# A two-layer hybrid decoder: part of the opening's modulation moved from VectorE to column tiles of TensorE

## The chip, the core and the metric

The kernel runs on one core of a Trainium2 chip. The core has five engines with a queue of instructions each: TensorE (PE, matmuls and, as PEld, their weight loads), VectorE (DVE), ScalarE (ACT), GpSimd (POOL) and SyncE (SP), which here mostly starts DMA transfers. The metric is device time in microseconds (us); lower is better.

## The reference

One sequence of 256 tokens with 2048 features goes through two layers. Each layer has six modulation vectors from a condition `c`, then a mixer (sliding-window attention beside an RWKV-7 recurrence) and a feed-forward part, each followed by a layer norm. Cut to what the change touches:

```python
cond = silu(c)                                                  # (1, 2048)
for l in range(2):
    mod = (cond @ w_ada[l] + b_ada[l]).reshape(1, 6, 1, 2048)   # 2048 x 12288 weights
    sh_m, sc_m, gt_m, sh_f, sc_f, gt_f = [mod[:, i] for i in range(6)]
    u = x * (1 + sc_m) + sh_m
    proj = u @ w_in[l]                                          # attention and RWKV columns
    ...
    mix = concat(y_attn, y_rwkv) @ w_out[l]
    x = layer_norm(alpha * x + gt_m * mix)
    u = x * (1 + sc_f) + sh_f
    ...                                                         # SwiGLU
    x = layer_norm(alpha * x + gt_f * ffn)
```

A modulation is thus a product of one row (2048 values of `cond`) with a matrix: 16 row steps of 128 rows each, all in f32.

## The kernel before, in words

**Weight products.** TensorE works on f32r pairs: `steps` (L414) loads a tile of weights as `raw`, splits it into `hi` (ACT, L430) and `lo` (DVE, L431), and `stream` (L452 to L455) or `tstream` (L464 to L466) issues three matmuls for each block. There are four `raw` tiles.

**The opening.** Nothing can be projected before the first two modulations, shift and scale of layer 0's mixer. `parts` (L1352) cuts the 2048 columns into five parts of 512, 512, 512, 256 and 256. For each, `ada_first` (L340) loads 16 row steps of both modulations at once (512 KB a step in the wide parts, 256 KB in the narrow ones, eight `ast` tiles in rotation) and adds them up on DVE: L351 for the first, L353 for the others (`acc = ast * cond + acc`, with a value of `cond` for each partition). `acc` then holds 128 partial sums for every column. `ada_sums` (L311) adds up the partitions: blocks of 128 columns are transposed on PE (L322), ACT sums each row of the result (L326, with the sum as a second output), and DVE adds the bias (L329). In the opening the transposes of both modulations take the same PSUM bank in turn, because `front` (L513) holds the other. `make_u` (L396) then transposes x (L404) and makes `u`, and `front` multiplies that part's columns with the weights of three groups of columns (`rk`, `lb` and eight blocks in `acc`).

**Later modulations.** `ada_steps` (L251) makes the other 20 units of 1024 columns, a few row steps at a time among the weight streams (L263 and L265 on DVE, then `ada_sums`). The two units of layer 0's mixer gate instead go through `ada_direct` (L276) while attention runs: each row step is a product on PE with `cond`'s 128 values broadcast to 32 columns, in four column tiles of 32, so that one bank collects four quarters of the row (L285, `gv`); ACT copies it (L299), two transposes bring it back to columns (L303), DVE adds the bias (L306).

**The mixer's order** is written out by hand in `ORDER`, one string for each layer: D, R, A, I, C, E are the steps of RWKV head group 0 to 3 (E ends with the group's two tiles of y), Q the attention projections, X opens the attention, a, b, c its three steps for each group of heads, w and z the output projection of attention and RWKV tiles. As long as `left` isn't empty, a finished y is written to DRAM (`keep_y`, L602); `have_y` (L612) brings it back through one tile `ysc`/`yf` (L616) and splits it (L509 on ACT, L510 on DVE). In layer 0 that holds for the tiles 8 to 11 (groups 0 and 1), fetched in z0 and z1.

Within these orders a planner, which simulates the engines, places the instructions of each queue. The constants' loads, the zero fills of `tinv` (L1379), the first `w2a2` (L644, L645) and the first rows of `ada_steps` (L261) have free tiles from the start and no order against the opening's rows.

Of the kernel before, what the change touches and what calls it, by code (L numbers as in the profile page):

```python
# [10 lines left out]
F32 = mybir.dt.float32  # L11
# [8 lines left out]
P = 128  # L20
# [21 lines left out]
    "D0 R0 A0 D1 I0 R1 C0 E0 Q1 A1 I1 D2 R2 A2 Q0 D3 C1 R3 E1 I2 A3 X Q2 a0 a1 b0 C2 a2 b1 c0 E2 a3 c1 I3 b2 b3 c2 c3 w0 C3 w1 w2 E3 z0 z1 z2 z3 w3",  # L42
    "D0 R0 A0 D1 R1 I0 C0 Q2 E0 A1 I1 D2 R2 A2 D3 Q1 C1 R3 E1 A3 I2 Q0 X a0 a1 b0 b1 c0 C2 I3 a2 b2 E2 a3 c1 b3 c2 c3 w0 C3 z0 w1 w2 E3 z1 z2 z3 w3",
)
PARTS = (4, 4, 4, 2, 2)
LAG = 2
WB = (4, 3, 2)
RED = 1
# [17 lines left out]
IDLE = {"ada": 0, "first": 0, "dec": (0, 0), "ffn": (11, 6), "mix": 8}  # L66
# [3 lines left out]
def hybrid_trunk_kernel(  # L70
# [92 lines left out]
    def prm(l, nm, i, n=1):  # L163
        o = PC[nm] + i
        return par[l][:, o // P, o % P:o % P + n]
# [5 lines left out]

    def setup(sp, l, half, behind=None):
# [78 lines left out]
    def ada_steps(l, mod, c0):  # L251

        src = w_ada[l].rearrange("(j p) n -> p j n", p=P)
        n0 = mod * D + c0
        if direct[0]:
            yield from ada_direct(l, mod, c0, src[:, :, n0:n0 + 1024])
            return
        acc = adap.tile([P, 1024], F32, tag="aacc", name="aacc")
        for j in range(KT):
            t = adap.tile([P, 1024], F32, tag="ast", name="ast", bufs=2)  # L260
            dma(t, src[:, j, n0:n0 + 1024])  # L261
# [12 lines left out]
        yield  # L274

    def ada_direct(l, mod, c0, src):  # L276
# [24 lines left out]
        b = bank()  # L301
        for i in range(2):
            PE.transpose(b[:, i * P:(i + 1) * P], row[:, i * P:(i + 1) * P], ident)  # L303
        col = mod * KT + c0 // P
        bv = b[:, 0:T].rearrange("p (i q r) -> p q i r", q=4, r=32)
        V.scalar_tensor_tensor(mods[l][:, col:col + 8].rearrange("p (q i) -> p q i", q=4), bv[:, :, :, 0], 1.0 if mod in (1, 4) else 0.0,  # L306
                               prm(l, "b_ada", col, 8).rearrange("p (q i) -> p q i", q=4), ALU.add, ALU.add)
# [3 lines left out]
    def ada_sums(l, mod, c0, blocks, idle=0):  # L311

        col = mod * KT + c0 // P
        n = len(blocks)
        sm = adap.tile([P, 8], F32, tag="asum", name="asum", bufs=2)
        for q in range(0, n, 4):
            b = bank()
            if q == 0:
                warm(b, idle)
            m = min(4, n - q)  # L320
            for i in range(m):
                PE.transpose(b[:, i * P:(i + 1) * P], blocks[q + i], ident)  # L322
            for i in range(m):
                bi = b[:, i * P:(i + 1) * P]
                if RED:
                    S.activation(bi, bi, AF.Copy, accum_out=sm[:, q + i:q + i + 1])  # L326
            if not RED:
                V.reduce_sum(sm[:, q:q + m], b[:, 0:m * P].rearrange("p (i k) -> p i k", k=P), axis=AX.X)
        V.scalar_tensor_tensor(mods[l][:, col:col + n], sm[:, 0:n], 1.0 if mod in (1, 4) else 0.0,  # L329
                               prm(l, "b_ada", col, n), ALU.add, ALU.add)  # L330
        if mod in (2, 5):
            row = adap.tile([8, P], F32, tag="arow", name="arow", bufs=2)[0:n]
            rb = bank()
            PE.transpose(rb[0:n, 0:P], mods[l][:, col:col + n], ident)
            S.copy(row, rb[0:n, 0:P])
            dma(gates[l, mod // 3, c0 // P:c0 // P + n], row)
# [3 lines left out]
    def ada_first(pool, c0, w):  # L340
# [3 lines left out]
        jj = 512 // w  # L344
        for j0 in range(0, KT, jj):
# [3 lines left out]
            for j in range(jj):  # L349
                if j0 + j == 0:  # L350
                    V.tensor_scalar_mul(acc, t[:, j], cond[:, 0:1])  # L351
                else:
                    V.scalar_tensor_tensor(acc, t[:, j], cond[:, j0 + j:j0 + j + 1], acc, ALU.mult, ALU.add)  # L353
            yield
        for m in range(2):
            ada_sums(0, m, c0, [acc[:, m, i * P:(i + 1) * P] for i in range(w // P)], IDLE["ada"] if m == 0 and c0 + w == D else 0)

# [182 lines left out]
    def mixer(l, us, mixp, feeds):  # L540
# [99 lines left out]
        def decays(g):  # L640
# [3 lines left out]
            dma(w2a2[0:64, :], rwkv_w2[l, :, gsl])  # L644
            dma(w2a2[64:128, :], rwkv_a2[l, :, gsl])  # L645
# [428 lines left out]
        for op in ORDER[l].split():  # L1074
# [9 lines left out]
            elif op[0] == "I":  # L1084
                invert(n, st[n], nscr[n])
            elif op[0] == "C":
# [262 lines left out]
    with tc.tile_pool(name="pro", bufs=1) as pp:  # L1349
        xv = x[0].rearrange("(t p) d -> p t d", p=P)  # L1350

        def parts():  # L1352
# [25 lines left out]
            for t in tinv:  # L1378
                dma(t.rearrange("e s t -> (e s t)").rearrange("(p n) -> p n", p=P), zt)  # L1379
# [38 lines left out]
```

## Time and profile before

| | us |
|---|---|
| median of 3 runs (2666.31 to 2670.81) | 2669.09 |
| profiled execution, its own time | 2671.02 |
| its span | 2669.0 |
| PE busy | 2518.3 |
| DVE busy | 1803.2 |
| ACT busy | 1186.1 |

The granted TensorE clock of the profiled execution was 0.974 on the mean. In a timeline's row stand the start, the duration, engine, line, operation, output and inputs, shape, the count of merged instructions and, in brackets, idle time before it with what ended it. In a row of waits: who waited for whom, the total in us, how often, and the longest. Starts are us from the span's start.

### The profile page before, as it was taken

What the parts mean: (1) busy time and instruction counts of PE and PEld (TensorE: products, weight loads), DVE (VectorE), ACT (ScalarE), POOL (GpSimd) and SP (SyncE); (2) the same over time, 40 slices, a digit from 0 to 9 for tenths busy, and PEclk for the clock granted to TensorE, in tenths of its full rate; (3) what the DMA queues carried; (4) which work ended last, traced back from release to release, by engine and by line L of the source; (5) the groups of instructions that cost most, each with busy time, mean ns of one, the idle gap of its engine ahead of it and who ended that gap; (6) DMA issues with size and microseconds to landing.
All of it is one profiled execution on the core that took longest, in us unless ns stands there. A gap on an engine that the chain in (4) does not pass through costs nothing.

```text
span 2669.0 us, 42270 instructions
## 1 busy us (share of the span) xinstructions
PE 2518.3 (94%) x15619; PEld 2090.0 (78%) x15619; DVE 1803.2 (68%) x2439; ACT 1186.1 (44%) x2023; POOL 147.2 (6%) x368
## 2 busy tenths in 40 slices
PE   3798998999999999999999999989899999999997
PEld 3797885677788888788888877867788888888887
DVE  7977766578777777676788776565855455545456
ACT  2464454335444444444444544544444443344442
POOL 1002122000000000000000023120000000000000
PEclk9899998999999999999999999989999999999999
DMA  9977668688998889888878685425655655566654
GB/s 370 361 214 250 198 186 264 204 327 294 326 337 297 302 303 314 292 301 298 300 250 304 196 274 160 121 58 185 218 188 186 194 186 194 195 191 188 192 188 147
DMA packets 336384, 637.51 MB, mean 239 GB/s; under 512 B 59510, under 2 KB 126514, under 8 KB 334642
## 3 DMA queue, kind: packets, MB, share of 16 engines
q1 hardware_dynamic: 333170, 629.05, 71.2%
q0 software_dynamic: 1280, 2.62, 0.4%
q10 hardware_dynamic: 1728, 3.15, 0.3%
q8 instruction: 122, 2.00, 0.3%
q14 instruction: 84, 0.69, 0.1%
HBM read 622.08 MB, written 12.62 MB: 238 GB/s over the span
## 4 chain that ended last, share of the span: by engine, by line
PE 76%; DMA 12%; DVE 6%; ACT 2%; issue 2%; POOL 1%; SPq 0%; DVEq 0%; ACTq 0%; POOLq 0%
PE acc L453 19%; PE acc L452 19%; PE acc L455 19%; DMA ast<-in_w_ada_dram 6%; PE acc L466 3%; PE acc L465 2%; PE acc L464 2%; DMA raw<-in_w_gate_up_dram 2%; DVE lo L431 2%; DVE aacc L265 1%; PE acc L977 1%; PE m L801 1%; PE mb L1288 1%; DMA raw<-in_w_in_dram 1%; PE aa L733 1%
## 5 line engine op out<-in xcount | busy, mean ns | idle before, releaser
L430 ACT CAST hi<-raw 128x1024 fp32r<-128x1024 f32 (+2 forms) x728 | 758.0, 1044 | 1078.8 <-PE acc L455 816.7
L431 DVE TENSOR_TENSOR lo<-raw,hi 128x1024 fp32r<-128x1024 f32 (+2 forms) x728 | 879.0, 1211 | 501.7 <-PE acc L453 342.8
L453 PE MATMUL acc<-lo,u 128*128 128x512 f32 x1568 | 514.9, 395 | 11.9 <-DVE lo L431 11.9
L455 PE MATMUL acc<-hi,u 128*128 128x512 f32 x1568 | 506.2, 391 | 0.0
L452 PE MATMUL acc<-hi,u 128*128 128x512 f32 x1568 | 459.3, 394 | 2.1 <-ACT sg L1281 1.6
L265 DVE SCALAR_TENSOR_TENSOR aacc<-ast,cond,aacc 128x1024 f32<-128x1024 f32 x270 | 345.4, 1279 | 115.7 <-DMA ast<-in_w_ada_dram 114.4
L453 PEld LDWEIGHTS acc<-lo,u 128*128 128x128 f32 x1568 | 293.1, 189 | 79.3 <-DVE lo L431 20.0
L452 PEld LDWEIGHTS acc<-hi,u 128*128 128x128 f32 x1568 | 295.2, 189 | 65.5 <-ACT sg L1281 2.5
L455 PEld LDWEIGHTS acc<-hi,u 128*128 128x128 f32 x1568 | 295.0, 188 | 61.7 <-issue 0.3
L453 PE MATMUL acc<-lo,ht 128*128 128x512 f32 (+1 forms) x720 | 243.9, 378 | 3.1 <-DVE lo L431 3.0
L455 PE MATMUL acc<-hi,ht 128*128 128x512 f32 (+1 forms) x720 | 242.2, 375 | 0.0
L452 PE MATMUL acc<-hi,ht 128*128 128x512 f32 (+1 forms) x720 | 217.0, 376 | 0.0
L464 PE MATMUL acc<-u,hi 128*128 128x256 f32 x720 | 200.9, 287 | 1.4 <-ACT hi L430 1.4
L465 PE MATMUL acc<-u,hi 128*128 128x256 f32 x720 | 201.1, 287 | 0.0
L466 PE MATMUL acc<-u,lo 128*128 128x256 f32 x720 | 188.9, 289 | 4.0 <-DVE lo L431 3.8
L453 PEld LDWEIGHTS acc<-lo,ht 128*128 128x128 f32 x720 | 134.9, 188 | 30.1 <-DVE lo L431 6.4
L455 PEld LDWEIGHTS acc<-hi,ht 128*128 128x128 f32 x720 | 135.6, 188 | 24.3
L452 PEld LDWEIGHTS acc<-hi,ht 128*128 128x128 f32 x720 | 134.7, 188 | 24.4
L464 PEld LDWEIGHTS acc<-u,hi 128*128 128x128 f32 x720 | 139.9, 194 | 4.4 <-issue 1.8
L465 PEld LDWEIGHTS acc<-u,hi 128*128 128x128 f32 x720 | 139.6, 194 | 2.8 <-issue 1.6
L466 PEld LDWEIGHTS acc<-u,lo 128*128 128x128 f32 x720 | 130.8, 193 | 8.9 <-DVE lo L431 5.7
L1128 POOL TENSOR_TENSOR brs<-brs,mhalf 128x1 f32<-128x1 f32 x8 | 7.1, 893 | 1713.1 <-DVE brs L1127 777.6
(358 smaller groups left out, 2943.6 us busy)
## 6 DMA issues: line engine op xcount, KB each, us to landing
ast<-in_w_ada_dram SPq DMA_DIRECT2D x368, 512.0 KB
raw<-in_w_gate_up_dram SPq DMA_DIRECT2D x704, 256.0 KB
raw<-in_w_down_dram SPq DMA_DIRECT2D x176, 512.0 KB
raw<-in_w_in_dram SPq DMA_DIRECT2D x82, 512.0 KB
raw<-in_w_out_dram SPq DMA_DIRECT2D x64, 512.0 KB
raw<-in_w_in_dram SPq DMA_DIRECT2D x120, 256.0 KB
ast<-in_w_ada_dram SPq DMA_DIRECT2D x32, 256.0 KB
lnw<-in_ln_w_dram SPq DMA_DIRECT2D x4, 1024.0 KB
```

The costliest lines, as they stand in the source:

```text
L265: ins = V.scalar_tensor_tensor(acc, t, cond[:, j:j + 1], acc, ALU.mult, ALU.add)
L430: S.copy(h, fl)
L431: ins = V.tensor_tensor(r, fl, h.bitcast(F32), ALU.subtract)
L452: PE.matmul(bt, lhsT=xh, rhs=hi[:, c0:c0 + w], start=st, stop=False)
L453: PE.matmul(bt, lhsT=xh, rhs=lo[:, c0:c0 + w], start=False, stop=False)
L455: PE.matmul(banks[t][q][:, 0:w], lhsT=xl, rhs=hi[:, c0:c0 + w], start=False, stop=sp_)
L464: PE.matmul(bt, lhsT=hi[:, c0:c0 + w], rhs=xh, start=st and opens, stop=False)
L465: PE.matmul(bt, lhsT=hi[:, c0:c0 + w], rhs=xl, start=False, stop=False)
L466: PE.matmul(bt, lhsT=lo[:, c0:c0 + w], rhs=xh, start=False, stop=sp_ and closes)
L733: PE.matmul(aas[h][:, cc * P:(cc + 1) * P], lhsT=bkc[hs, cc, :], rhs=ar[hs, cc, :], start=True, stop=True)
L801: PE.matmul(m1[BH[i], e * CH:(e + 1) * CH], lhsT=st[i]["am"][e // NCH][BH[i], e % NCH, 0:CH], rhs=yt[BH[i], e, :], start=True, stop=True)
L977: PE.matmul(sbs[par_][:, j * w:(j + 1) * w], lhsT=qT[hs, j, n * P:(n + 1) * P], rhs=kT[hs, 0:w], start=True, stop=True)
```

## The change

Each part of the opening adds 12 of its 16 row steps on DVE as before; the last four are products on PE in four column tiles of 32, into the bank `gv`. When both are done, `ones` products add the 128 partitions of `acc` to that bank, ACT copies the row of it, transposes bring it to columns and DVE adds the bias of both modulations. This sum by ones also takes the place of transposes and ACT sums in the 18 later units made on DVE (8 transposes and 8 ACT sums each before; 4 products, one copy and 2 transposes after). Besides:

- `fetch` puts the first `w2a2` loads, the zero fills of `tinv` and the first two row loads of `ada_steps` behind the last row load of the opening;
- layer 0's order fetches the parked y early (`y0` after E2, `y1` after I3);
- layer 1's order has C2 and I3 ahead of a2, `b1` after a2, `b2` after c1, and z0 after E3.

```diff
 ORDER = (
-    "... X Q2 a0 a1 b0 C2 a2 b1 c0 E2 a3 c1 I3 b2 b3 c2 c3 w0 C3 w1 w2 E3 z0 z1 z2 z3 w3",
-    "... X a0 a1 b0 b1 c0 C2 I3 a2 b2 E2 a3 c1 b3 c2 c3 w0 C3 z0 w1 w2 E3 z1 z2 z3 w3",
+    "... X Q2 a0 a1 b0 C2 a2 b1 c0 E2 y0 a3 c1 I3 y1 b2 b3 c2 c3 w0 C3 w1 w2 E3 z0 z1 z2 z3 w3",
+    "... X a0 a1 b0 C2 I3 a2 b1 c0 E2 a3 c1 b2 b3 c2 c3 w0 C3 w1 w2 E3 z0 z1 z2 z3 w3",
 )
+ROWS_PE = {512: 4, 256: 4}
...
+    def fetch(dst, src, later=True):
+        ins = dma(dst, src)
+        if later:
+            tc.add_manual_dep(ins.ins, lead[0], order, reason="behind the first modulation rows")
...
 (ada_steps)
-            dma(t, src[:, j, n0:n0 + 1024])
+            fetch(t, src[:, j, n0:n0 + 1024], j < 2 and not done)
...
-        ada_sums(l, mod, c0, [acc[:, i * P:(i + 1) * P] for i in range(8)])
+        ada_sums(l, c0, acc, (mod,), 8)
+        if mod in (2, 5):
+            gate_row(l, mod, c0, 8)
...
+    def row_blocks(acc, w):
+        return [acc[:, q // 2, q % 2 * w:(q % 2 + 1) * w] if len(acc.shape) == 3 else acc[:, q * w:(q + 1) * w] for q in range(4)]
+
+    def add_rows(gv, t, w, weights, first, last):
+        for q, blk in enumerate(row_blocks(t, w)):
+            PE.matmul(gv[32 * q:32 * q + 32, 0:w], lhsT=weights.to_broadcast([P, 32]), rhs=blk, start=first, stop=last)
+
+    def ada_sums(l, c0, acc, mods_, n, gv=None):
+        w = len(mods_) * n * P // 4
+        first = gv is None
+        if first:
+            gv = bank()
+        add_rows(gv, acc, w, ones, first, True)
+        row = row_blocks(acc, w)[0]
+        S.copy(row, gv[:, 0:w])
+        place(l, c0, row, mods_, w)
+
+    def place(l, c0, row, mods_, w):
+        b, m = bank(), w // P
+        for i in range(m):
+            PE.transpose(b[:, i * P:(i + 1) * P], row[:, i * P:(i + 1) * P], ident)
+        bv = b[:, 0:w].rearrange("p (i q r) -> p q i r", q=4, r=32)
+        nq = 4 // len(mods_)
+        for k, mod in enumerate(mods_):
+            col = mod * KT + c0 // P
+            V.scalar_tensor_tensor(mods[l][:, col:col + nq * m].rearrange(...), bv[:, k * nq:(k + 1) * nq, :, 0],
+                                   1.0 if mod in (1, 4) else 0.0, prm(l, "b_ada", col, nq * m).rearrange(...), ALU.add, ALU.add)
...
 (ada_first)
+        cut = KT - ROWS_PE[w]
+        gv = None
...
-                if j0 + j == 0:
+                k = j0 + j
+                if k >= cut:
+                    gv = gv or bank()
+                    add_rows(gv, t[:, j], w // 2, cond[:, k:k + 1], k == cut, False)
+                elif k == 0:
                     V.tensor_scalar_mul(acc, t[:, j], cond[:, 0:1])
...
-        for m in range(2):
-            ada_sums(0, m, c0, [acc[:, m, i * P:(i + 1) * P] for i in range(w // P)], ...)
+        ada_sums(0, c0, acc, (0, 1), w // P, gv)
...
 (decays)
-            dma(w2a2[0:64, :], rwkv_w2[l, :, gsl])
-            dma(w2a2[64:128, :], rwkv_a2[l, :, gsl])
+            fetch(w2a2[0:64, :], rwkv_w2[l, :, gsl], l + g == 0)
+            fetch(w2a2[64:128, :], rwkv_a2[l, :, gsl], l + g == 0)
...
+            elif op[0] == "y":
+                have_y([8 + 2 * n, 9 + 2 * n])
...
-                dma(t.rearrange("e s t -> (e s t)").rearrange("(p n) -> p n", p=P), zt)
+                fetch(t.rearrange("e s t -> (e s t)").rearrange("(p n) -> p n", p=P), zt)
```

`ada_direct` ends in `place` too, and `gate_row` is the end of the old `ada_sums` (one transpose, a copy and a store for the gates), moved into a function.

More of the change, by code (lines that the diff above doesn't have):

```diff
@@ L41 @@
 ORDER = (
[L42 to L43 removed]
+    "D0 R0 A0 D1 I0 R1 C0 E0 Q1 A1 I1 D2 R2 A2 Q0 D3 C1 R3 E1 I2 A3 X Q2 a0 a1 b0 C2 a2 b1 c0 E2 y0 a3 c1 I3 y1 b2 b3 c2 c3 w0 C3 w1 w2 E3 z0 z1 z2 z3 w3",
+    "D0 R0 A0 D1 R1 I0 C0 Q2 E0 A1 I1 D2 R2 A2 D3 Q1 C1 R3 E1 A3 I2 Q0 X a0 a1 b0 C2 I3 a2 b1 c0 E2 a3 c1 b2 b3 c2 c3 w0 C3 w1 w2 E3 z0 z1 z2 z3 w3",
 )
 PARTS = (4, 4, 4, 2, 2)
+ROWS_PE = {512: 4, 256: 4}
 LAG = 2
 WB = (4, 3, 2)
[L48 removed]
 AR = (3, 7)
@@ L65 @@
 TWO_PI = 2.0 * math.pi
-IDLE = {"ada": 0, "first": 0, "dec": (0, 0), "ffn": (11, 6), "mix": 8}
+IDLE = {"first": 0, "dec": (0, 0), "ffn": (11, 6), "mix": 8}
 @with_exitstack
@@ L300, in ada_direct @@
         turn[:] = 1, 1
[L301 to L307, printed above, removed]
+        place(l, c0, row, (mod,), T)
@@ L308, in ada_direct @@
         done.add((l, mod, c0 // 1024))
         yield
-    def ada_sums(l, mod, c0, blocks, idle=0):
-        col = mod * KT + c0 // P
[L314 to L336, printed above, removed]
@@ new lines, in place @@
+    def place(l, c0, row, mods_, w):
[6 more added lines that the diff above has]
+            col = mod * KT + c0 // P
+            V.scalar_tensor_tensor(mods[l][:, col:col + nq * m].rearrange("p (q i) -> p q i", q=nq), bv[:, k * nq:(k + 1) * nq, :, 0],
+                                   1.0 if mod in (1, 4) else 0.0,
+                                   prm(l, "b_ada", col, nq * m).rearrange("p (q i) -> p q i", q=nq), ALU.add, ALU.add)
@@ L338, in hybrid_trunk_kernel, with gate_row @@
+    def gate_row(l, mod, c0, n):
+        col = mod * KT + c0 // P
+        row = adap.tile([8, P], F32, tag="arow", name="arow", bufs=2)[0:n]
+        rb = bank()
+        PE.transpose(rb[0:n, 0:P], mods[l][:, col:col + n], ident)
+        S.copy(row, rb[0:n, 0:P])
+        dma(gates[l, mod // 3, c0 // P:c0 // P + n], row)
     lead = []
@@ L349, in ada_first @@
             for j in range(jj):
-                if j0 + j == 0:
+                k = j0 + j
[3 more added lines that the diff above has]
+                elif k == 0:
                     V.tensor_scalar_mul(acc, t[:, j], cond[:, 0:1])
                 else:
-                    V.scalar_tensor_tensor(acc, t[:, j], cond[:, j0 + j:j0 + j + 1], acc, ALU.mult, ALU.add)
+                    V.scalar_tensor_tensor(acc, t[:, j], cond[:, k:k + 1], acc, ALU.mult, ALU.add)
             yield
-        for m in range(2):
-            ada_sums(0, m, c0, [acc[:, m, i * P:(i + 1) * P] for i in range(w // P)], IDLE["ada"] if m == 0 and c0 + w == D else 0)
+        ada_sums(0, c0, acc, (0, 1), w // P, gv)
     done = set()
```

## The prediction

> **What bounds the kernel now.** I read the page first, then the stages, then the waits of each stage.
>
> ```profile
> span 2669.0 us, 42270 instructions
> PE 2518.3 (94%) x15619; PEld 2090.0 (78%) x15619; DVE 1803.2 (68%) x2439; ACT 1186.1 (44%) x2023; POOL 147.2 (6%) x368
> ```
>
> TensorE (PE) is busy for all but 151 us, so a change pays where it takes PE's waits away or starts PE sooner. The largest loss is the opening; its stages follow (columns: PE, weight loads, DVE, ACT, POOL busy us with counts, granted clock, DMA share, GB/s).
>
> ```profile
> 60.00:100.00 40.00, 27.63 (x206) 25.76 (x205) 37.53 (x38) 14.96 (x33) 0.00 (x0) 0.89 1.05 392
> 100.00:130.00 30.00, 27.17 (x189) 26.14 (x190) 27.74 (x45) 15.76 (x43) 0.00 (x0) 0.81 1.04 341
> 134.60:162.50 27.90, 27.85 (x227) 27.58 (x227) 15.72 (x31) 15.12 (x31) 1.03 (x4) 0.94 0.63 176
> 44.00:162.50 118.50, 98.55 (x727) 94.71 (x727) 98.26 (x132) 53.12 (x118) 1.03 (x4) 0.90 0.94 321
> ```
>
> To 130 us the DMA is full and DVE works 65.3 of 70 us; from 134.6 PE has no gap and the DMA is at 0.63. PE's front runs from 44 to 162.5 us: 727 instructions at 27.85/227 = 0.123 us need 89 us, so 29 us are lost, 20 idle and the rest to a clock of 0.90. What PE waited for there:
>
> ```profile
> PE mb L322 <- DVE aacc L353: 8.7, 2, 4.6
> PE mb L404 <- ACT mb L326: 5.2, 3, 1.7
> PE lb L464 <- ACT u L410: 2.2, 2, 1.1
> PE mb L322 <- ACT mb L326: 1.7, 1, 1.7
> ```
>
> 15.6 us of the 20 are waits on the modulation: its row sum on DVE, and the column sums on ACT.
>
> ```profile
> 128.24 6.26 DVE L353 SCALAR_TENSOR_TENSOR aacc<-ast,cond,aacc 128x512 f32<-128x512 f32 x8
> 134.65 0.41 PE L322 MATMUL mb<-ident,aacc 128*128 128x128 f32 x2 [4.12 <-DVE aacc L353]
> 144.59 0.38 PE L322 MATMUL mb<-ident,aacc 128*128 128x128 f32 x2
> ```
>
> At the end DVE is the one that lags: eight rows back to back, with PE's queue standing 4.12 us at the transposes, though the full DMA stage ended at 130. The second modulation's transposes follow only at 144.6.
>
> **The change part by part.** *Row steps to PE.* DVE's rows of the opening:
>
> ```profile
> L353 DVE SCALAR_TENSOR_TENSOR aacc<-ast,cond,aacc 128x1024 f32<-128x1024 f32 x45 | 57.7, 1282 | 7.9 <-DMA ast<-in_w_ada_dram 7.4
> ...
> L353 DVE SCALAR_TENSOR_TENSOR aacc<-ast,cond,aacc 128x512 f32<-128x512 f32 x30 | 22.5, 749 | 0.7 <-DVE mods L329 0.2
> ```
>
> DVE loses 12 x 1.28 + 8 x 0.75 = 21.4 us. PE gains 20 product rows of four column tiles. The direct unit of layer 0 issues the same form, 256 columns wide:
>
> ```profile
> 443.90 0.64 PE L285 MATMUL gv<-ast,cond 128*32 128x256 f32 x8
> 444.46 0.72 PE L977 MATMUL acc<-qT 64*128 64x128 f32 x8
> ...
> 485.65 1.50 PE L285 MATMUL gv<-ast,cond 128*32 128x256 f32 x24
> 487.08 0.71 PE L836 MATMUL mr<-bkt,ah 64*128 64x128 f32 x4
> ```
>
> One row of four tiles (eight records) holds PE 0.56 us alone and 1.43/3 = 0.48 in a run. The 12 wide rows cost 12 x 0.56 = 6.7. The 8 rows of 128 columns have no row: half to all of 0.56; nearer to half, as the work is halved, so 0.35 and 2.8. With five sums by ones (3 x 0.56 + 2 x 0.35 = 2.4) and eight row transposes (1), that is 13 us.
>
> *Sums.* Old and new forms:
>
> ```profile
> 36.29 1.12 PE L322 MATMUL mb<-ident,aacc 128*128 128x128 f32 x4 [20.86 <-DVE aacc L353]
> 41.92 1.11 PE L404 MATMUL mb<-ident,xt 128*128 128x128 f32 x4 [1.72 <-ACT mb L326]
> ```
>
> ```profile
> L299 ACT COPY grow<-gv x2: 372/372/372, 467.5 to 517.5; 128x256 f32<-128x256 f32 x2
> L303 PE MATMUL mb<-ident,grow x4: 271/272/273, 469.5 to 522.3; 128*128 128x128 f32 x4
> ```
>
> ```profile
> 734.89 1.04 PE L322 MATMUL mb<-ident,aacc 128*128 128x128 f32 x8
> 735.69 0.71 PE L453 MATMUL acc<-lo,u 128*128 128x512 f32 x2
> ```
>
> Eight transposes hold PE 0.80 us, so the opening's 32 give back 3.2: PE's work rises by 13 - 3.2 = about 10 us, from 89 to 99. From the last DVE row to the transposes of x the old sum takes 41.92 - 36.29 = 5.6 us, because both modulations go through one bank in turn; the new one is a product (0.64), a copy (0.37), two overlapping transposes (0.27 each) and two small DVE steps, with handoffs about 2.3, an estimate. That saves 3.3 us at each of five sums. The 18 later units trade 0.80 us of transposes for one sum (0.56) and two transposes (0.2): nothing on PE, -0.2 to +0.3 each, and 3 us less of ACT, which does not bound those stages. New is that the two transposes wait for an ACT copy; the L303 row, the same pair, showed no wait of PE. I take +1 for all 18 (bounds -4 to +5).
>
> *Transfers moved behind the last opening row:*
>
> ```profile
> 24.23 0.35 SPq L1379 DMA_DIRECT2D tinv<-zt  x1
> ...
> 30.02 0.81 SPq L261 DMA_DIRECT2D ast<-in_w_ada_dram  x2
> ...
> 41.62 0.34 SPq L261 DMA_DIRECT2D ast<-in_w_ada_dram  x1
> ```
>
> ```profile
> ast<-in_w_ada_dram SPq DMA_DIRECT2D x56, 512.0 KB
> ...
> tinv<-zt SPq DMA_DIRECT2D x2, 260.0 KB
> ```
>
> Three rows of the next unit (the third needs the first one's buffer), two zero fills and two small loads: 1.57 + 0.53 and some 0.1 = 2.2 MB, 5.6 us of a full DMA at 390 GB/s. They go to where the DMA is at 0.63: of 28 us some 10 are free, so I charge nothing. Without that cover they would push the last w_in tiles back by 5.6 us. On SP they were ahead of opening rows; now only w_in tiles stand behind them.
>
> *Opening, sum.* The first matmul moves from 44 to about 44 - 5.6 - 3.3 = 35. Work is 99. Of the 29 lost I expect 20: the DVE waits (8.7) mostly go, as DVE no longer lags and the products fill the gap ahead of each sum; the ACT waits shrink by half. The front would end at 35 + 99 + 20 = 154 instead of 162.5. Bounds: with all 29 still lost 163 (no gain), with the modulation's 15.6 all gone 148 (-14). I take -8. What is late next is PE itself.
>
> The Trainium skill ("TensorE: Matmul & The Clock Gate", What's actually happening) says that the array runs at half clock by default and at full clock only after about 3.4 us of activity. The rows agree in kind (0.81 and 0.89 before 130 us). By that rule products in idle gaps would also save clock, and the front would end some 5 us sooner than this sum.
>
> *The early y0 and y1 of layer 0.* Heads 0 and 1 were parked in DRAM; the kernel fetches them just as PE wants them:
>
> ```profile
> 531.11 5.32 SPq L616 DMA_DIRECT2D yf<-yd  x2
> ...
> 530.65 0.50 PE L452 MATMUL acc<-hi,yl 128*128 128x512 f32 x1 [2.31 <-ACT yl L509]
> ...
> 535.67 0.50 PE L452 MATMUL acc<-hi,yl 128*128 128x512 f32 x1 [0.42 <-ACT yl L509]
> ...
> 538.72 0.50 PE L452 MATMUL acc<-hi,yl 128*128 128x512 f32 x1
> ...
> 544.45 0.53 PE L452 MATMUL acc<-hi,yl 128*128 128x512 f32 x1 [2.72 <-ACT yl L509]
> ...
> 548.90 0.39 PE L452 MATMUL acc<-hi,yl 128*128 128x512 f32 x1
> ```
>
> Idle 2.31 + 0.42 + 2.72 = 5.4 us. The twelve matmuls after the second, short wait take 538.72 - 535.67 = 3.05 us; those after the first take 535.67 - 0.42 - 530.65 = 4.6 and those after the last 548.90 - 544.45 = 4.45, so 3 more go to the slow clock: 8.4 us in all, bounds 0 and -8.4. Hoisting puts four casts, four subtractions and four loads (each waiting for one buffer, on SP among the direct unit's row loads) into the attention, where PE waits on chains: +1. I take -7 and +1.
>
> *Order of layer 1.* I3 and C2 move ahead of a2 and b1, z0 to the end. Waits there that this could touch:
>
> ```profile
> PE m L808 <- issue: 2.1, 1, 2.1
> PE m L801 <- DVE den L1000: 1.6, 1, 1.6
> ```
>
> I take -1 of these 3.7, with +3 as the other bound: z0 no longer fills PE between C3 and w1.
>
> *Sum:* -8 - 7 + 1 + 1 - 1 = -14. The profiled execution took 2671.0 us (span 2669.0 and 2 around it), 1.9 above the median of 2669.1. 2671 - 14 = 2657, from the median 2655; I forecast **2656**. PE is the busy engine after the opening (94% of the span), so what is won there should stay.
>
> **The rivals.** *The opening gives nothing.* Products stand in PE's in-order queue until their row lands, 1.35 us apart (0.52 MB at 390 GB/s). If PE stops for the four landings of the parts 2 and 3, 8 x 1.35 = 10.8 us, what was idle is idle again. Behind them stand the w_in matmuls of the part before and the sum, for which ACT's u waits. For it: the DMA is full. Against it, the direct unit's waits for its row loads, 0.6 us at most:
>
> ```profile
> PE gv L285 <- DMA ast<-in_w_ada_dram: 1.5, 3, 0.6
> ```
>
>  Its time: 2656 + 8 = 2664.
>
> *The y waits stay*, because the planner or the single buffer leaves the loads late: 2656 + 7 = 2663.
>
> *The clock follows the work:* the front regains the 9 us of slow clock too, 2656 - 7 = 2649.
>
> *Slower: PE stands at the row copy.* In each of the 18 units the two transposes may wait for the copy (0.37) behind a cast on ACT:
>
> ```profile
> L430 ACT CAST hi<-raw 128x1024 fp32r<-128x1024 f32 (+2 forms) x728 | 758.0, 1044 | 1078.8 <-PE acc L455 816.7
> ```
>
> 18 x (0.37 + 1.04) = 25 us, 2681. It outweighs the gain from 0.8 us per unit on. Against it: the L303 pair without a wait, and the planner has weight products to put between.
>
> **How the numbers follow.** Forecast 0.55, opening nothing 0.18, y waits stay 0.08, clock 0.11, copy 0.08. The range is 2644 to 2668: the lower end is the clock rival with the upper bounds of the y and layer 1 terms, the upper end the opening rival with the +4 of later units; beyond it lies the slower rival. A difference under 0.2% (5.3 us) can't be told from none. Forecast and clock fall on faster, the two partial rivals lie at that bound, and the copy on slower: 0.77 faster, 0.15 same, 0.08 slower.
>
> **What would show it.** The last opening row on DVE before 126 us and no wait of PE on it over 2 us; the front's end near 154; no wait on yl before z0 and z1; transposes after a row copy with no idle time before them. It is wrong if PE idles ahead of gv products in the opening, if the front ends after 160, or if ACT copies head PE's waits.

## The result and the profile after

The changed kernel took **2687.5 us** (median of 7 runs, 2676.8 to 2696.5), the kernel before 2666.3 beside it (7 runs). The ratio is 1.0070 (95% interval 1.0052 to 1.0088): some 19 us **slower**, where the prediction had 2656 and a range up to 2668. Below, ratios are turned into us with 2667 us, about the kernel before in every comparison.

The page of the profiled execution after:

```profile
span 2686.0 us, 42325 instructions
...
PE 2535.2 (94%) x15831; PEld 2083.2 (78%) x15831; DVE 1782.3 (66%) x2419; ACT 1137.1 (42%) x1694; POOL 147.3 (5%) x368
```

DVE and ACT lost work as planned (21 and 49 us), PE's busy time grew by 17, and so did the span. To see where, the spans of both traces are cut into five stages: the opening up to the end of the last product on the `lb` columns; layer 0's mixer up to the first product of its feed-forward part; that part up to the first product of layer 1's front; layer 1's front and mixer; the second feed-forward part and the end.

| us | opening | mixer 0 | feed-forward 0 | mixer 1 | feed-forward 1 | span |
|---|---|---|---|---|---|---|
| before | 157.4 | 465.9 | 768.0 | 526.3 | 751.4 | 2669.0 |
| after | 151.4 | 475.1 | 780.2 | 526.1 | 753.2 | 2686.0 |
| difference | -6.0 | +9.2 | +12.2 | -0.2 | +1.8 | +17.0 |

**The opening** came out about as forecast (-6.0 for -8). Stages of after, then of before (columns as in the prediction's table of stages), cut from the first product to the last on the `lb` and `rk` columns:

```profile
38.30:151.70 113.40, 99.46 (x828) 87.98 (x828) 79.38 (x108) 41.00 (x64) 0.99 (x4) 0.94 0.96 347
```

```profile
44.00:157.70 113.70, 93.75 (x686) 90.03 (x686) 93.90 (x125) 48.76 (x110) 1.03 (x4) 0.89 0.95 330
```

The stage starts 5.7 us sooner and is as long as before: 142 more instructions on PE, but 14 us idle instead of 20 and a clock of 0.94 instead of 0.89. DVE's last rows in after stand at

```profile
114.65 4.68 DVE L375 SCALAR_TENSOR_TENSOR aacc<-ast,cond,aacc 128x512 f32<-128x512 f32 x6
```

and PE's waits between 38 and 152 us are short:

```profile
PE lb L485 <- ACT u L431: 3.7, 3, 1.5
PE acc L485 <- ACT hi L451: 2.6, 2, 1.4
PE mb L425 <- DVE mods L341: 2.4, 2, 2.0
PE mb L319 <- ACT u L431: 2.1, 1, 2.1
```

The DVE row sum, 8.7 us of waits before, is gone from the list.

**The first feed-forward stage** is where the forecast saw next to nothing and 12 us went. The stretch from 640 to 1390 us lies within it in both. After, and then before:

```profile
640.00:1390.00 750.00, 733.76 (x3383) 595.23 (x3382) 563.25 (x551) 308.13 (x347) 0.00 (x0) 1.00 0.88 303
```

```profile
640.00:1390.00 750.00, 740.26 (x3443) 610.50 (x3442) 572.06 (x569) 334.96 (x514) 1.08 (x2) 1.00 0.89 305
```

PE does less work in the same time, at a full clock in both. Its waits in that stretch, and those of DVE, after:

```profile
PE acc L474 <- DVE lo L452: 16.1, 16, 3.0
...
DVE aacc L270 <- DMA ast<-in_w_ada_dram: 84.1, 55, 4.0
```

and before:

```profile
PE acc L453 <- DVE lo L431: 7.6, 15, 1.7
...
DVE aacc L265 <- DMA ast<-in_w_ada_dram: 74.6, 50, 3.4
```

So DVE stands longer at rows of the later units whose load hasn't landed, the `lo` splits queue behind those rows, and PE waits for `lo`. One such place in after, as SP, DVE and PE rows of the timeline:

```profile
1140.58 0.33 SPq L173 DMA_DIRECT2D ast<-in_w_ada_dram  x1
1141.72 0.80 SPq L443 DMA_DIRECT2D raw<-in_w_gate_up_dram  x2
1144.36 4.71 SPq L173 DMA_DIRECT2D ast<-in_w_ada_dram  x2
1149.88 1.94 SPq L443 DMA_DIRECT2D raw<-in_w_gate_up_dram  x4
```

```profile
1143.05 1.28 DVE L270 SCALAR_TENSOR_TENSOR aacc<-ast,cond,aacc 128x1024 f32<-128x1024 f32 x1 [0.16 <-DMA ast<-in_w_ada_dram]
1147.43 1.28 DVE L270 SCALAR_TENSOR_TENSOR aacc<-ast,cond,aacc 128x1024 f32<-128x1024 f32 x1 [3.10 <-DMA ast<-in_w_ada_dram]
1148.64 2.35 DVE L452 TENSOR_TENSOR lo<-raw,hi 128x1024 fp32r<-128x1024 f32 x2
```

```profile
1149.91 1.22 PE L474 MATMUL acc<-lo,u 128*128 128x512 f32 x2 [3.03 <-DVE lo L452]
```

Two row loads stand in a pair on SP, where mostly one row load stands between weight loads; the weight loads behind them are issued only at 1149.88. This is the longest such wait, and not a measure of the whole: between 640 and 1390 us there are 8 such pairs after and 4 before, and how a late unit comes to each of them wasn't followed.

**Why the rows are late** can be read at the seam of two units. After (a tile's instructions: count, min/median/max ns, first and last start):

```profile
L319 PE MATMUL mb<-aacc,ones x8: 379/390/403, 1014.5 to 1014.8; 128*32 128x256 f32 x8
...
L336 PE MATMUL mb<-ident,aacc x2: 270/270/271, 1020.7 to 1020.8; 128*128 128x128 f32 x2
L329 ACT COPY aacc<-mb x1: 373/373/373, 1015.2 to 1015.2; 128x256 f32<-128x256 f32 x1
L268 DVE TENSOR_SCALAR aacc<-ast,cond x1: 744/744/744, 1021.5 to 1021.5; 128x1024 f32<-128x1024 f32 x1
```

The sum is done at 1015 and copied at 1015.2, **into `aacc` itself** (`row = row_blocks(acc, w)[0]`). The two transposes that read the row stand behind weight products on PE until 1020.7, and the first row of the next unit, which overwrites `aacc`, follows at 1021.5. Before, the eight transposes read `aacc` and it is free:

```profile
L322 PE MATMUL mb<-ident,aacc x8: 272/272/273, 1006.3 to 1007.1; 128*128 128x128 f32 x8
...
L263 DVE TENSOR_SCALAR aacc<-ast,cond x1: 745/745/745, 1009.4 to 1009.4; 128x1024 f32<-128x1024 f32 x1
```

In 16 of the 17 seams of after the next unit's first row starts 0.1 to 2.1 us after the end of these two transposes. Over all 17, the median time from the end of a unit's last row on DVE to the start of the next unit's first (the **gap**, below) is 12.8 us after and 7.8 before. That is theory H. Its rivals: O, the new orders and the deferred transfers disturb layer 0's mixer; S, the `ones` products themselves cost; R, the planner places all queues anew after any edit, and that alone moves the time.

### The profile page after: what moved, and what is told of

Same layout as the page of the kernel before. It is cut to its first block, busy times and chain, and to the rows that moved or that the text cites. A ratio compares the mean times of both kernels' runs of the same rounds, so it can differ in the third digit from the quotient of the medians.

```text
span 2686.0 us, 42325 instructions
## 1 busy us (share of the span) xinstructions
PE 2535.2 (94%) x15831; PEld 2083.2 (78%) x15831; DVE 1782.3 (66%) x2419; ACT 1137.1 (42%) x1694; POOL 147.3 (5%) x368
## 4 chain that ended last, share of the span: by engine, by line
PE 62%; DMA 5%; DVE 5%; POOL 2%; issue 1%; ACT 1%; SPq 0%; DVEq 0%; POOLq 0%; ACTq 0%
PE acc L474 17%; PE acc L476 17%; PE acc L473 17%; DMA ast<-in_w_ada_dram 2%; DVE lo L452 2%; PE acc L487 2%; PE acc L485 1%; PE acc L486 1%; DVE aacc L270 1%; POOL tmp L806 1%; PE mb L1311 1%; POOL ttl L808 1%; DMA raw<-in_w_gate_up_dram 1%; DMA raw<-in_w_out_dram 0%; DMA raw<-in_w_in_dram 0%
```

## The experiments

Each was timed beside the kernel before. `unit_sums` in a diff is a sum for the later units alone. "Changed kernel" is the one with the whole change.

**1. The units' old sums in the changed kernel.**

```diff
-        ada_sums(l, c0, acc, (mod,), 8)
+        unit_sums(l, mod, c0, [acc[:, i * P:(i + 1) * P] for i in range(8)])
```

> The changed kernel is 19 us (0.7%) slower than the one before. Here its 18 later units sum up as before again (eight transposes, eight ACT sums); opening, orders and deferred transfers stay changed. Theory H (held accumulator): the summed row is copied into the accumulator itself, so the only aacc tile stays taken from the ones product until the row's transposes, 3.5 to 6.2 us where a unit was looked at, and the next unit's rows, its loads and the lo splits behind them on DVE come late. Then this run loses the 19 us and keeps the 6 us of the opening and most of the 8 us of the y hoist: 8 to 14 us under the kernel before. Theory O (the new orders and the deferred transfers disturb layer 0's mixer and what follows): nothing comes back, still 15 to 23 us over before. Theory R (every edit makes the planner place all queues afresh, and no part owns the loss): somewhere between, 0 to 15 over before, with the loss in other places.

2669.5 us, ratio 1.0017 (0.9999 to 1.0035), +4.5 us. Feed-forward 0 is back at 764.4, the gap at 8.4. Some 14 us are returned, but H's number is missed: the gains of opening and y do not show, and the result lies where R had put it.

**2. The row in a tile of its own.** The two small tiles of the gate rows became one of 1 KB a partition, which both uses share.

```diff
-        row = row_blocks(acc, w)[0]
+        row = adap.tile([P, T], F32, tag="arow", name="srow", bufs=1) if first else row_blocks(acc, w)[0]
 (gate_row)
-        row = adap.tile([8, P], F32, tag="arow", name="arow", bufs=2)[0:n]
+        row = adap.tile([P, T], F32, tag="arow", name="arow", bufs=1)[0:n, 0:P]
```

> The changed kernel, but in the later units the row is copied into a tile of its own (the 1 KB that the two gate rows had; they share it now), so the accumulator is free after the ones product. Theory H: as in the run with the old unit sums within 5 us, 5 to 14 us under the kernel before, and DVE's first row of a unit no longer waits for the transposes of the unit before. Theory S (the ones products themselves cost: PE stands in order at them until DVE's last row is done): no better than the changed kernel, 15 to 23 us over before. Theories O and R: within 8 us of the changed kernel, 11 to 27 over before.

2668.5 us, 1.0010 (0.9997 to 1.0023), +2.7: 16 us under the changed kernel with the same instructions, and within 5 us of run 1 as H expected; that it would be under the kernel before is missed again. The seam of the same two units, `aacc` and then the row's tile:

```profile
L319 PE MATMUL mb<-aacc,ones x8: 379/390/403, 1003.5 to 1003.7; 128*32 128x256 f32 x8
...
L268 DVE TENSOR_SCALAR aacc<-ast,cond x1: 748/748/748, 1006.7 to 1006.7; 128x1024 f32<-128x1024 f32 x1
```

```profile
L336 PE MATMUL mb<-ident,srow x2: 270/270/271, 1009.7 to 1009.8; 128*128 128x128 f32 x2
```

The transposes still come 6 us after the product, but the next unit's first row no longer waits for them; it starts 3 us ahead of them, and ahead of their end in 16 of the 17 seams. The gap is 6.0 us, and PE's wait in the stretch of 640 to 1390 us is back where it was:

```profile
PE acc L474 <- DVE lo L452: 7.0, 12, 1.1
...
DVE aacc L270 <- DMA ast<-in_w_ada_dram: 58.4, 45, 3.5
```

S falls: the `ones` products are all there. So does the thought that PE's 17 us more of busy time are more work: with the same 15831 instructions it is 2516.0 us here, less than before. O falls as the cause of the 16 us, since the new orders and the deferral are all there too.

**3. Both old orders in the changed kernel.**

```diff
-    "... c0 E2 y0 a3 c1 I3 y1 b2 ..."
+    "... c0 E2 a3 c1 I3 b2 ..."
...
-    "... b0 C2 I3 a2 b1 c0 E2 a3 c1 b2 ... w0 C3 w1 w2 E3 z0 z1 ..."
+    "... b0 b1 c0 C2 I3 a2 b2 E2 a3 c1 ... w0 C3 z0 w1 w2 E3 z1 ..."
```

> The changed kernel with both layers' orders as before (no early y, layer 1's steps as they were). Theory H: the y waits come back, so 5 to 9 us slower than the changed kernel, 24 to 30 over before. Theory O: 10 to 20 us faster than the changed kernel, 0 to 9 over before. Theory R: within 8 us of the changed kernel either way, without the loss being tied to a stage.

2682.9 us, 1.0066 (1.0046 to 1.0086), +17.6: no different from the changed kernel. Feed-forward 0 takes 781.1, the gap is 12.8. For the orders O falls (the deferral is still there, see 8); the y gain that H expected to go missing isn't seen in the total.

**4. The early y alone, in the kernel before.**

```diff
-    "... c0 E2 a3 c1 I3 b2 ..."
+    "... c0 E2 y0 a3 c1 I3 y1 b2 ..."
```

> The kernel before with one part of the change alone: y0 after E2 and y1 after I3 in layer 0's order. The prediction had -7 for the waits and +1 for the early work: 4 to 8 us under before under theory H. Theory O (the loads and splits in the attention disturb it, as the changed kernel loses some 9 us at 400 to 440 us): 0 to 8 us over before. Theory R: anywhere within 8 us, with shifts in stages where nothing was edited.

2662.5 us, 0.9987 (0.9976 to 0.9998), -3.5, a little short of the 4 to 8 that H expected. In its trace the first product of the output projection (a `w`) comes 4.0 us later than before, and from there to the last one it takes 105.2 us instead of 109.3: the one takes up the other, and mixer 0 is only 0.9 us shorter.

**5. The units' sums by ones alone, in the kernel before, row in `aacc`.**

```diff
-        ada_sums(l, mod, c0, [acc[:, i * P:(i + 1) * P] for i in range(8)])
+        unit_sums(l, mod, c0, acc)
...
+            PE.matmul(gv[32 * q:32 * q + 32, 0:T], lhsT=ones.to_broadcast([P, 32]), rhs=acc[:, q * T:(q + 1) * T], start=True, stop=True)
+        row = acc[:, 0:T]
+        S.copy(row, gv[:, 0:T])
```

> The kernel before with one part of the change alone: the 18 later units are summed by ones, and the row is copied into the accumulator. The two runs that freed the accumulator came within 4 us of the kernel before, where the changed kernel is 19 over. Theory H (held accumulator): this part alone makes the whole loss, 14 to 20 us over before, and the median time from a unit's last row on DVE to the next unit's first is some 5 us longer than before (12.8 in the changed kernel against 7.8). Theory R (the planner's new placing, or this sum only together with the other edits): -4 to 8.

2683.1 us, 1.0056 (1.0041 to 1.0072), +15: this part alone makes most of the loss. The gap is 11.8.

**6. The same with the row in its own tile.**

```diff
-        row = acc[:, 0:T]
+        row = adap.tile([P, T], F32, tag="arow", name="srow", bufs=1)
```

> The kernel before with the later units summed by ones, the row in a tile of its own. With the row in the accumulator this edit alone came out 15 us over before. Theory H (the held accumulator is the price, the sums by ones are free): within 4 us of before, and the median time between two units' rows back at 6 to 8 us. If the ones products or the row copy have a price of their own on PE (0.57 us of product, 0.2 of transposes, 18 times): 5 to 15 over.

2666.4 us, 0.9996 (0.9985 to 1.0007), -1. The gap is 6.3. The sums by ones cost nothing, as forecast; the tile does.

**7. The opening's products and sums alone, in the kernel before** (later units, orders and transfers as before).

```diff
+                if k >= cut:
+                    gv = gv or bank()
+                    add_rows(gv, t[:, j], w // 2, cond[:, k:k + 1], k == cut, False)
...
-        for m in range(2):
-            ada_sums(0, m, c0, ...)
+        ada_sums(0, c0, acc, (0, 1), w // P, gv)
```

> The opening's part alone: the last four row steps of each part as products and its sums by ones; later units, orders and transfers as before. The prediction had -8 for the opening with the deferred transfers, and that what is won there stays. Theory K (it stays): 4 to 8 us under before. Theory G (it is given back in layer 0's mixer, where the changed kernel's lead of 6 us at 160 us was gone by 425 us): within 3 us of before, with w0's first product no earlier.

2664.9 us, 1.0000 (0.9987 to 1.0013). The first product starts 4.2 us sooner, the last `lb` product ends at 156.6 instead of 157.4: the lead is gone within the opening.

**8. The deferral alone, in the kernel before.**

```diff
-            dma(t, src[:, j, n0:n0 + 1024])
+            fetch(t, src[:, j, n0:n0 + 1024], j < 2 and not done)
...
-            dma(w2a2[0:64, :], rwkv_w2[l, :, gsl])
+            fetch(w2a2[0:64, :], rwkv_w2[l, :, gsl], l + g == 0)
```

> The kernel before with the deferral alone. In the traces so far the last product on the lb columns ends at 157.4 us before, 151.4 in the changed kernel, 156.6 with products and sums but no deferral, and 149.9 with deferral and sums but no products. Theory T (the transfers moved back are what wins in the opening, the product rows win nothing): that end comes to 150 to 154 here, and the time is 2 to 8 us under before. If products and deferral only help together: the end stays at 156 to 158 and the time within 3 us.

2676.3 us, 1.0035 (1.0020 to 1.0050), **+9**. The opening ends at 152.6, as theory T expected, but the total goes the other way: mixer 0 takes 470.6, feed-forward 0 771.4 and mixer 1 533.6.

**9. The row in its own tile, without the deferral.**

```diff
-        if later:
+        if False:
```

> The changed kernel with the row in a tile of its own (2.6 us over before in the last call), and without the deferral: tinv's zero fills, the first w2a2 and the first rows of the later units are free to go early again. Theory D (the deferral makes the first unit late and costs the mixer of layer 0 what the opening won): 4 to 10 us under before. Theory K: the 2.2 MB push the opening back by up to 5.6 us, 3 to 8 us over before. Theory G: within 3 us of the run with the deferral, 0 to 5 over before.

2681.8 us, 1.0061 (1.0038 to 1.0084), +16; none of the theories had that. The trace is of a long execution (2696 us). In it mixer 0 takes 22 us more than before (487.9) and mixer 1 some 5 more; half of the 22 are lost at one place. PE and DVE there:

```profile
457.82 0.70 PE L894 MATMUL db<-uv,bkt 128*64 128x64 f32 x8 [11.79 <-DVE rh L873]
```

```profile
456.39 0.71 DVE L818 STREAM_TRANSPOSE ytr<-tm 128x512 f32<-128x512 f32 x1 [11.49 <-DMA tm<-tinv]
457.02 0.38 DVE L871 TENSOR_TENSOR mt<-mr,mt 128x256 f32<-128x256 f32 x1
457.33 0.34 DVE L873 TENSOR_TENSOR rh<-mr,ar 128x192 f32<-128x192 f32 x1
```

DVE stands 11.5 us at a transpose of the next head group's inverse, whose blocks come back from DRAM, with the small step that PE wants two instructions behind it. Nothing in the edit concerns these instructions; they are placed in another order. In 2 the same transpose waits as long, but behind the two steps:

```profile
430.68 0.34 DVE L873 TENSOR_TENSOR rh<-mr,ar 128x192 f32<-128x192 f32 x1
442.70 0.71 DVE L818 STREAM_TRANSPOSE ytr<-tm 128x512 f32<-128x512 f32 x1 [11.68 <-DMA tm<-tinv]
```

There no single wait of PE between 160 and 620 us is longer than 3.8 us.

**10. The row in its own tile, no product rows in the opening.**

```diff
-ROWS_PE = {512: 4, 256: 4}
+ROWS_PE = {512: 0, 256: 0}
```

> The changed kernel with the row in a tile of its own, and with no product rows in the opening (all 16 row steps on DVE, sums by ones). If the products make the opening's gain and it stays (K): 3 to 8 us slower than with them, 5 to 11 over before, and the front ends some 6 us later. If the gain comes from the shorter sums and the deferral: within 2 us of the run with them. Theory G: within 3 us, though the front ends later.

2664.3 us, 0.9981 (0.9970 to 0.9993), **-5**: faster than with the products (2), against all three expectations. The opening ends at 149.9.

**11. The same with layer 1's order as before.**

```diff
-    "D0 R0 A0 D1 R1 ... a0 a1 b0 C2 I3 a2 b1 c0 E2 a3 ..."
+    "D0 R0 A0 D1 R1 ... a0 a1 b0 b1 c0 C2 I3 a2 b2 E2 a3 ..."
```

> The fastest so far (changed kernel, row in its own tile, no product rows; 5 us under before), now with layer 1's order as before. The prediction had -1 for that order, with +3 as the other bound. If it costs (z0 no longer fills PE between C3 and w1): 2 to 4 us faster than with it, 7 to 9 under before. If it gains as forecast: 0 to 2 slower, 3 to 5 under. Theory R (placing): within 5 either way, with no change at C3 and w1.

2663.6 us, 0.9984 (0.9972 to 0.9995), -4: no difference.

**12. Two product rows instead of four, row in its own tile.**

```diff
+ROWS_PE = {512: 2, 256: 2}
```

> The changed kernel with the row in its own tile, with two product rows a part instead of four (2.6 us over before) or none (5 under). If each product row has a price (it stands in PE's queue until its transfer lands, and adds 0.56 us of work): between the two, 0 to 3 under before, with the front's last lb product between 149.9 and 154.1. Theory R: outside that by more than 4 us, and the difference not in the opening.

2668.4 us, 1.0000 (0.9990 to 1.0011). The opening ends at 148.8, a little under the expected band; the total lies between the neighbours.

**13. Product rows in the two narrow parts alone, row in its own tile.**

```diff
+ROWS_PE = {512: 0, 256: 4}
```

> The changed kernel with the row in its own tile, and product rows in the two narrow parts of the opening alone, where the kernel before stood 4.1 us at DVE's last rows. If products pay where DVE lags and cost where it doesn't: the last lb product ends at 147 to 150 us, and the time is 5 to 9 us under before. If they cost everywhere: 150 to 154, and 0 to 4 under.

2665.9 us, 0.9993 (0.9982 to 1.0005), -2. The opening ends at 148.9; mixer 1 takes 534.6, 8 us more than before, and the total shows nothing of the 5 to 9 us that were expected.

**14. No work changed: two of the opening's constant sets in the other order.**

```diff
-            for l, half in ((0, 1), (1, 0), (1, 1)):
+            for l, half in ((1, 0), (0, 1), (1, 1)):
```

> The kernel before with an edit that takes no work away and adds none: two of the opening's constant sets are read in the other order. Theory R (the planner places the mixers' queues afresh after any edit in the opening, and that alone moves the time by some us): 3 to 10 us from before in either direction, with the difference in the mixers and not in the feed-forward stage. Theory C (each edit's own cost, as worked out, makes the differences): within 2 us of before.

2687.7 us, 1.0077 (1.0061 to 1.0093), **+21**, twice R's own bound and as much as the whole change. Opening 157.6, feed-forward 0 765.0; mixer 0 takes 488.6 instead of 465.9. PE's longest waits there:

```profile
PE mb L322 <- DVE aacc L265: 12.8, 1, 12.8
PE acc L958 <- DVE qr L951: 6.9, 1, 6.9
PE acc L453 <- DVE lo L431: 6.8, 6, 3.1
PE m L801 <- DVE ytr L797: 6.3, 1, 6.3
```

The first is a unit's sum, which stands at the head of PE's queue while DVE still waits for that unit's rows.

**15. No work changed: the units' pace in layer 0's mixer.**

```diff
-AP = (0.65, 0.3)
+AP = (0.64, 0.3)
```

> The kernel before with the pace of the later units in layer 0's mixer at 0.64 a weight step instead of 0.65: the same instructions, some a weight step later. Theory R: 3 to 10 us from before in either direction, the difference in layer 0's or layer 1's mixer. Theory C: within 2 us.

2678.1 us, 1.0037 (1.0024 to 1.0050), +10, again in mixer 0 (475.4).

**16. The early y and the units' sums with their own tile, in the kernel before** (4 and 6 together).

```diff
+    "... c0 E2 y0 a3 c1 I3 y1 b2 ..."
...
+        unit_sums(l, mod, c0, acc)
...
+        row = adap.tile([P, T], F32, tag="arow", name="srow", bufs=1)
```

> The kernel before with the two parts of the change that cost nothing alone: the early y (3.4 us under before) and the units' sums by ones with a row tile of their own (1 us under). If they add up: 3 to 6 us under before. Theory R: anywhere within 8 us.

2664.1 us, 0.9988 (0.9975 to 1.0002), -3: they add up within what can be told.

**17 and 18. The held accumulator under another placing.** The edit of 15 in the changed kernel, and in the kernel of 2, which differs by the row's tile alone.

```diff
-AP = (0.65, 0.3)
+AP = (0.64, 0.3)
```

> The changed kernel with the pace of the later units in layer 0's mixer at 0.64 instead of 0.65, which changes no work and places the mixers anew. By the stages of the traces so far: from the first product of the first feed-forward stage to the first of layer 1's front, the three kernels that hold the row in the accumulator take 774 to 781 us, the fifteen others 763 to 771; layer 0's mixer takes 461 to 488 without a tie to either. Theory H: the feed-forward stage at 774 to 781 again, whatever the mixer does. If the feed-forward stage too depends on the placing: 763 to 770 in this kernel or over 774 in its twin with the row in its own tile.

> The twin: the changed kernel with the row in its own tile, and the same pace of 0.64. Theory H: the feed-forward stage at 763 to 770 us, 8 to 15 below its twin; layer 0's mixer anywhere between 461 and 488. If the placing sets the feed-forward stage: over 774 here, or no difference to the twin.

Row in `aacc`: 2686.3 us, 1.0074 (1.0054 to 1.0095), +20, feed-forward 0 782.9, gap 11.4. Row in its own tile: **2658.3 us, 0.9970 (0.9956 to 0.9983), -8**, feed-forward 0 764.0, gap 5.0. PE's wait between 640 and 1390 us, first and second:

```profile
PE acc L474 <- DVE lo L452: 18.4, 24, 2.0
```

```profile
PE acc L474 <- DVE lo L452: 5.7, 7, 1.3
```

The feed-forward stages come out near where H put them (774 to 781 and 763 to 770), and 19 us apart, more than the 8 to 15 that were expected. The second is the fastest kernel of this study and beats both that it began with.

**All traces by stage:**

| us | opening | mixer 0 | feed-forward 0 | gap | time against before |
|---|---|---|---|---|---|
| row held in `aacc`: changed kernel | 151.4 | 475.1 | 780.2 | 12.8 | +19 |
| 3 old orders | 154.4 | 472.5 | 781.1 | 12.8 | +18 |
| 5 units alone | 156.8 | 477.9 | 774.2 | 11.8 | +15 |
| 17 other pace | 152.5 | 473.3 | 782.9 | 11.4 | +20 |
| not held: before | 157.4 | 465.9 | 768.0 | 7.8 | 0 |
| 1 old sums | 156.2 | 467.2 | 764.4 | 8.4 | +4 |
| 2 own tile | 154.1 | 466.5 | 766.8 | 6.0 | +3 |
| 4 y alone | 158.1 | 465.0 | 765.9 | 7.6 | -3 |
| 6 units, own tile | 157.1 | 466.0 | 765.4 | 6.3 | -1 |
| 7 opening alone | 156.6 | 468.1 | 762.9 | 7.9 | 0 |
| 8 deferral alone | 152.6 | 470.6 | 771.4 | 7.5 | +9 |
| 9 own tile, no deferral | 154.9 | 487.9 | 768.3 | 6.4 | +16 |
| 10 own tile, no products | 149.9 | 463.4 | 764.7 | 6.2 | -5 |
| 11 the same, old layer 1 | 150.8 | 467.1 | 762.7 | 6.1 | -4 |
| 12 own tile, two rows | 148.8 | 462.9 | 768.4 | 6.3 | 0 |
| 13 own tile, narrow parts | 148.9 | 468.3 | 765.8 | 6.2 | -2 |
| 14 no work changed, setup | 157.6 | 488.6 | 765.0 | 7.8 | +21 |
| 15 no work changed, pace | 157.0 | 475.4 | 767.1 | 8.0 | +10 |
| 16 y and units, own tile | 158.7 | 460.9 | 763.4 | 6.0 | -3 |
| 18 own tile, other pace | 149.6 | 463.4 | 764.0 | 5.0 | -8 |

Each row of stages is one execution, from 8 us below (1) to 14 above (9) the median of its kernel: of two kernels with the same instructions in the opening, one (2) ends it at 154.1 and the other (18) at 149.6. The first feed-forward stage separates cleanly all the same: 774 to 783 us in the four kernels that hold the row in `aacc`, 763 to 771 in the sixteen others, the two without a change of work among them. Mixer 0 does not: it runs from 461 to 489 among the sixteen.

## Why the prediction was wrong

**The failed step** is "The 18 later units trade 0.80 us of transposes for one sum (0.56) and two transposes (0.2): nothing on PE", with its +1 (bounds -4 to +5). It followed what the instructions cost and not what the copied row occupies. Timed alone, the term came to +15 (5), and to -1 with a tile of its own (6). The instruction prices were right: at the median, a unit's sum holds PE 0.57 us up to the next instruction, its two transposes 0.14. These are the rows of after, which also count the overlap with their neighbours and the opening (groups by line and shape; time, then mean ns, then idle time before them):

```profile
L319 PE MATMUL mb<-aacc,ones 128*32 128x256 f32 x168 | 14.9, 413 | 3.9 <-DVE aacc L270 3.9
```

```profile
L336 PE MATMUL mb<-ident,aacc 128*128 128x128 f32 x44 | 9.7, 301 | 1.0 <-ACT aacc L329 1.0
```

But the sum ends with a copy into the only accumulator, so from the product to the transposes no row of the next unit can be added. Before, eight transposes read `aacc` itself and freed it at once. The diff showed it in one line, `row = row_blocks(acc, w)[0]`; the question left out was which tile the new wait keeps, and who wants that tile next. Measured alone (5 against 6) the held tile costs 16 us, in the whole change (changed kernel against 2) 16, under another placing (17 against 18) 28. Of these, 9 to 19 us are in feed-forward 0. Mixer 0 is 9 to 12 us longer in all three pairs too; the first units run there, but the placing by itself moves that stage as much, so this part is not shown.

The Trainium skill ("Perfetto Trace Analysis", Optimization Strategy) says that the same gap coming back through a stretch of a kernel can mean that no buffer is free for the next tile. The seams of after are that gap, 5 us longer than before at the median, though on DVE's rows and not on the engine that is to be kept busy.

**The rival "PE stands at the row copy"** gave 2681 and came nearest in time, for a wrong reason: PE waits 1.0 us in all for that copy (row L336 above), not 25. Its chance of 0.08 was for a mechanism that doesn't occur.

**The opening** (forecast -8, bounds 0 to -14): -6.0 in the trace of after. Its parts were misjudged. The first product starts at 38.3, not 35: the moved transfers were to bring 5.6 us of that, and alone they bring 1.7 at most (8: 42.4, where the seven kernels that leave the opening's work as it was have 43.4 to 44.1); the shorter sum, put at 3.3, brings 3.1 more (10 against 8). The product rows hold about the prices that were given (0.46 to 0.57 us a wide row after the first part), but nothing shows that they win: with four of them and the deferral the opening ends at 149.6 to 156.2 (six kernels), with none at 149.9 and 150.8, without the deferral at 154.9 and 156.6, and with the deferral and the old sums at 152.6. Those seven kernels end it at 156.8 to 158.7. So by itself the deferral brings the end of the opening forward, and products with sums don't (7); but 2 and 9, which differ in the deferral alone, end it at 154.1 and 154.9, so what it does beside four product rows isn't shown. "The products fill the gap ahead of each sum" gained nothing that can be told.

**"The opening gives nothing"**: not within the opening of after, where PE waits for no `ast` at a product row after the first product. One such row stands 2.1 us for ACT's `u` (the row `PE mb L319` above); that is the one place in the front where PE idles ahead of these products, which the prediction took for a sign of being wrong. Products without the deferral do give nothing (7), though PE waits for `ast` there for 0.6 us at most.

**The clock** (rival "the clock follows the work"): in the front it rose from 0.89 to 0.94. PE's busy time rose by 5.7 us, where 10 us of work were to be added, about 2 of them ahead of the first product. By the Trainium skill ("TensorE: Matmul & The Clock Gate", What's actually happening) activity releases the throttle, so products in idle gaps should have raised it. The trace agrees in kind, and so do the others: the ten kernels with product rows have 0.93 to 0.97 in the front, the ten without 0.83 to 0.92. But it wins no time that can be told: without any products (10) the opening ends as early at 0.92. (The rival named 9 us of slow clock and took off 7, without a reason.)

**The early y** (-7 and +1): the waits are gone as said. After, between 500 and 560 us, PE waits only

```profile
PE acc L473 <- ACT hi L451: 0.2, 1, 0.2
```

From the first to the last product of layer 0's output projection eleven of the twelve kernels with the early y take 101 to 107 us and one 97, the eight without it 107 to 114. The work put into the attention costs more than +1: alone (4), the projection starts 4.0 us later and is 4.1 shorter, so that mixer 0 gains next to nothing. Where the -3.5 of the whole comes from isn't shown; the largest difference of that trace, 4.4 us, is in mixer 1 (521.9 instead of 526.3), where nothing was edited. The rival "the y waits stay" falls.

**Layer 1's order** (-1): no difference (11 against 10), inside its bounds.

**"What is won there should stay"** is the second wrong sentence. It took PE's 94% as a bound. Layer 0's mixer is not bounded by PE's work alone: before, PE is busy 435 of its 466 us, against 757 of 768 in feed-forward 0. PE stands there for chains over DVE, POOL and DRAM, whose instructions the planner places anew after each edit. The changed kernel lost 9.2 us there in spite of the early y, with these waits of PE between 160 and 620 us, after and then before:

```profile
PE gv L292 <- DMA ast<-in_w_ada_dram: 7.2, 7, 1.9
PE mb L319 <- DVE aacc L270: 3.9, 1, 3.9
PE bnb L791 <- DVE bv L793: 2.9, 1, 2.9
```

```profile
PE acc L452 <- ACT yl L509: 5.4, 3, 2.7
PE m L801 <- DVE ytr L797: 4.8, 1, 4.8
PE acc L453 <- DVE lo L431: 3.7, 5, 1.5
```

The two kernels without a change of work lose 9.5 and 22.7 us in the same stage. Whether the 9.2 us are the held accumulator (its four kernels take 472 to 478) or the placing can't be told from these runs.

**Do the parts add up?** Timed alone, each in the kernel before, they are 0 for the opening's products and sums (7), +9 for the deferral (8), -3.5 for the early y (4) and +15 for the units' sums in `aacc` (5); layer 1's order made no difference (11 against 10). That is +20.5 for a measured +19, and without the held tile +4.5 for a measured +3 (2). So beside the held tile a second term failed: the opening with its deferred transfers, -8 in the forecast, is +9 by its parts. Why the deferral costs that stays open. It ends the opening 4.8 us sooner, and then mixer 0, feed-forward 0 and mixer 1 take 4.7, 3.4 and 7.3 us more.

The agreement may be luck. Taking the deferral out of 2 costs another 13 us (9) where it should give 9 back, and a pace that costs 10 us in the kernel before (15) brings 11 in 2 (18). The range of 24 us had no term for the placing, and the difference that the prediction took for the least that can be told, 0.2% (5.3 us), is less than what an edit without a change of work does to this kernel.

## What to carry to other kernels

When a sum, copy or eviction is rewritten, list for every tile it touches when it is taken and when it is freed, not only what the instructions cost: a result that is written back into its own source keeps the source until the last reader, and that reader may stand behind 5 to 6 us of other work in its engine's queue, as here. A tile of one kilobyte a partition for the row was worth 16 us here, and the gap between a unit's last step and the next unit's first is the number to look at.

Where a planner places the queues, time an edit that changes no work before you believe a difference of half a per cent, and compare by stages: a stage with a regular pattern (here feed-forward 0, 763 to 771 us without the fault) tells a cause apart where the total can't.

## What the runs showed that was not expected

Two edits that change no work cost 10 and 21 us, as much as any cost that the prediction worked out. The traces show how a placing gets so dear: one instruction at the head of a queue, waiting for data from DRAM itself or through DVE, holds 12 to 13 us of PE's time (9 and 14). In 9 the two small steps behind it needed no more than tiles that were there before DVE stood still (PE's `mr` by 442 us), and ran at 457.

Moving 2.2 MB of early transfers behind the opening's rows brought the end of the opening forward by 5 us alone, and up to 7.5 us together with the shorter sums, although the same bytes have to be loaded a little later. Alone it still cost the whole kernel 9 us (8): an end of one stage that comes sooner is not yet a gain.
